# Dense projections as 512-column products with the tokens stationary

## The chip, the cores and the metric

The kernel runs on one core of a Trainium2 chip. The core has TensorE (PE, matrix products into PSUM banks), VectorE (DVE), ScalarE (ACT), GpSimd (POOL) and SyncE (SP, whose queue issues the transfers from memory). Each engine takes its own instructions in order, and semaphores hold an instruction until what it reads is there and what it overwrites has been read. The metric is the device time of one launch in microseconds.

## The reference

A block of a diffusion model over 256 latent tokens of width 1024, with 256 context tokens. What the change touches is the token mixer behind the input projection:

```python
z = h @ w_in            # 9 sections of 1024: q, i, f_fwd, f_bwd, og, u, v, gate_a, gate_b
# chunk_mlp: v normalised over its 1024 columns, mixed over 128 positions by w_s, times u
mu = jnp.mean(vf, axis=-1, keepdims=True)
vn = (vf - mu) * lax.rsqrt(var + EPS)
s = jnp.einsum('gtp,bnpgc->bntgc', w_s, vn) + b_s.T[:, :, None]
y_b = u * s
y_a = rms_norm(o, gnorm_g) * jax.nn.silu(og)      # o: two gated linear recurrences, 8 heads
merged = (jax.nn.sigmoid(gate_a) * (y_a @ w_branch_a)
          + jax.nn.sigmoid(gate_b) * (y_b @ w_branch_b))
x = x + g1 * (merged @ w_out)
# then: modulated norm, top 4 of 32 experts (clamped SwiGLU, 1024 wide), residual, norm
```

u and v pass through an exact GELU. The expert weights are 32 x 3 x 1024 x 1024 numbers of float32, and all of them are read.

## The kernel before

The work stands in five stages: start (modulation, first projections), attention in four pairs of heads with dense products in the gaps (heads 0 to 7), the middle (v, u, branch_b, gate and branch_a, w_out), the router, and 32 experts.

A dense product of float32 is made of three: `split` (L264) has ScalarE round a block to fp32r (`hi`, `ghi`) and DVE subtract it (`lo`, `glo`), and `dense` (L332) adds hi*hi, lo*hi and hi*lo. The class `Granule` (L311) is one weight block of 1024 x 256 in a 1 MB slot, and its `parts` splits four of its eight row tiles at a time, 128 x 1024 elements, into one of three buffers. With `natural` false the weights are stationary and the result is [channel, token]; with `natural` true the tokens are stationary, the weights stream past, and the result is [token, channel]. Either way one product here has 256 columns, except where latent and context tokens stream together (512). `two` (L349) makes a whole Granule's result in one PSUM bank (`acc`, two buffers). The other banks are `tp` (two buffers), `scores`, `o_ps`, `ua` and `ub` (one each).

v (L633) is natural; gate_b (L576, called `mb`), u (L649), branch_b (L669), gate (L662) and branch_a (L695) are [channel, token], so that the gated sum `m` can go as it is into w_out as its stationary operand; w_out (L703) is natural, and each quarter of its result goes into the residual `acc` and, turned, into the router. `mb` is the branch-b gate, made in the gaps of the last pair of heads, then multiplied by branch_b's product.

Weights are loaded by SP in program order into a rotation of slots: three of 1 MB (`ring`), and, from the third v block on (`LATER = 3`, L626), three of 2 MB (`ringb`). A load waits until the splits have read what was in its slot, and every load behind it waits with it. The first expert weights follow w_out in this queue (L69, L73). Later the experts have more slots.

What lies where on each engine is set by a scheduler from the program's dependences; the products of the attention and of the middle stage may pass each other on TensorE. `keep_busy` (L180) issues bf16 products of 512 columns that nobody reads.

Of the kernel before, what the change touches and what calls it, by code (L numbers as in the profile page):

```python
# [8 lines left out]
F32 = mybir.dt.float32  # L9
F32R = mybir.dt.float32r  # L10
BF = mybir.dt.bfloat16
I32 = mybir.dt.int32
AF = mybir.ActivationFunctionType
# [3 lines left out]
P = 128  # L17
D = 1024
# [13 lines left out]
def kernel(  # L32
# [295 lines left out]

    def win(sec, j, pieces=False):
        return Granule(w_in[0, :, sec * D + j * 256:sec * D + (j + 1) * 256], pieces)  # L330
# [236 lines left out]
    for j in range(5):  # L567
# [6 lines left out]
        else:  # L574
            mb = consts.tile([P, KT, T], F32, name="mb", tag="d1")
            steps = [lambda i=i: sc.activation(mb[:, 2 * i:2 * i + 2], two(win(8, i), hT[0], False), AF.Sigmoid)  # L576
                     for i in range(4)] + [lambda: None]
# [54 lines left out]
    for j in range(4):  # L632
        pp = two(win(6, j), hT[0], True)  # L633
        more_slots(j + 1)
        sc.activation(v[:, :, j * 256:(j + 1) * 256], pp, AF.Gelu)
# [26 lines left out]
    def gate(j):  # L662
        pp = two(win(7, j), hT[0], False)
        t = mid.tile([P, 2, T], F32, name="t2", bufs=2)
        sc.activation(t, pp, AF.Sigmoid)
        return t

    for j in range(4):
        pp = two(Granule(w_branch_b[0, :, j * 256:(j + 1) * 256]), (ybh, ybl), False)  # L669
        ve.tensor_mul(mb[:, 2 * j:2 * j + 2], mb[:, 2 * j:2 * j + 2], pp)  # L670
# [22 lines left out]
    for j in range(4):  # L693
        t = gate(j)
        pp = two(Granule(w_branch_a[0, :, j * 256:(j + 1) * 256]), (yhi, ylo), False)  # L695
        m = mid.tile([P, 2, T], F32, name="t3", bufs=2)
        ve.tensor_mul(m, pp, t)
        ve.tensor_add(m, m, mb[:, 2 * j:2 * j + 2])
        split(m, mhi[:, 2 * j:2 * j + 2], mlo[:, 2 * j:2 * j + 2])
# [3 lines left out]
    for j in range(4):  # L703
        s = slice(j * 256, (j + 1) * 256)
        g = Granule(w_out[0, :, s])
        t = mid.tile([P, 2, 256], F32, name="t3", bufs=2)
        if j < 3:
            pp = two(g, (mhi, mlo), True)
            ve.tensor_mul(t, pp, view(g1bc, j * 256, [[0, 2], [1, 256]]))
            ve.tensor_add(acc[:, :, s], acc[:, :, s], t)  # L710
        else:
            pps = [bank("acc") for _ in range(2)]
            dense(g, [(pps[tt][:, 0], tt, (mhi, mlo), True) for tt in range(2)], True)
            for tt in range(2):
# [375 lines left out]
```

## Time and profile before

| | us |
|---|---|
| median of three runs | 1432.9 (1430.99 to 1435.51) |
| profiled execution | 1439.14 |
| its span | 1437.4 |
| TensorE busy in the span | 1341.1 (93%) |
| DVE, ScalarE, POOL busy | 615.9, 306.2, 171.8 |

In the profile's rows times are microseconds from the start of the span. A row of a timeline has the start, the duration, the engine, the line, the operation, out<-in with the names of the tiles, and how often it stands in a row; in brackets the idle time before it and what ended it. Consecutive matmuls overlap, so their pace is read from starts, not from durations. For a product the operand that streams stands first behind the arrow and the stationary one second: `acc<-hh,ghi` has the weights stationary, `acc<-ghi,hh` the tokens.

### The profile page before, as it was taken

The numbers are of one execution on the slowest core, as the hardware profiler recorded it, in microseconds if no ns is written. First come the engines' busy times: TensorE is split into PE (matmuls) and PEld (weight loads), VectorE is DVE, ScalarE is ACT, GpSimd is POOL, SyncE is SP. The second block draws the span as 40 slices with busy tenths as digits, with TensorE's granted clock in tenths as the row PEclk, the third lists the DMA queues.
The fourth block names the chain that finished last, engine by engine and source line by source line (L and its number), as shares of the span: only waits on it lengthen the run. The fifth ranks groups of instructions, "written<-read, shape, count | busy, mean of one in ns | idle before, by whom it ended". The sixth has DMA issues, their size and how long they took to land. (4 is left out here: it accounts for less than half of the span.)

```text
span 1437.4 us, 18504 instructions
## 1 busy us (share of the span) xinstructions
PE 1341.1 (93%) x7806; PEld 727.7 (51%) x7806; DVE 615.9 (43%) x1100; ACT 306.2 (21%) x494; POOL 171.8 (12%) x147
## 2 busy tenths in 40 slices
PE   6988898989999999999999999989999899898986
PEld 3887787788999843333333332323323233232322
DVE  5597777768768522322322323213222232222214
ACT  3472545365444310000000000000000000010001
POOL 3045434240064000000000000000000000000001
PEclk8999999999999999999999999999999999999998
DMA  9645252534984899999999999999999999999994
GB/s 333 193 147 173 98 200 92 173 125 162 325 256 175 344 418 411 427 424 425 425 424 427 427 424 426 423 428 426 425 426 423 427 426 426 425 424 426 426 424 156
DMA packets 106882, 487.37 MB, mean 339 GB/s; under 512 B 6277, under 2 KB 64778, under 8 KB 77098
## 3 DMA queue, kind: packets, MB, share of 16 engines
q1 hardware_dynamic: 105946, 483.37, 83.9%
q0 software_dynamic: 848, 2.75, 0.6%
q8 instruction: 63, 1.03, 0.3%
q14 instruction: 25, 0.20, 0.0%
HBM read 485.06 MB, written 1.05 MB: 338 GB/s over the span
## 5 line engine op out<-in xcount | busy, mean ns | idle before, releaser
L827 PE MATMUL gate<-w,xT 128*64 128x512 f32 x1024 | 269.1, 604 | 13.4 <-DMA w<-in_w_dram 13.0
L827 PE MATMUL lin<-w,xT 128*64 128x512 f32 x1024 | 263.0, 592 | 0.0
L864 PE MATMUL py<-w,hT 128*64 128x512 f32 x992 | 227.2, 605 | 26.0 <-DMA w<-in_w_dram 25.9
L883 DVE SCALAR_TENSOR_TENSOR acc<-sc,wts,acc 128x512 f32<-128x512 f32 x122 | 86.0, 747 | 206.1 <-PE sc L880 206.1
L346 PE MATMUL acc<-hh,glo 128*128 128x256 f32 (+1 forms) x480 | 150.1, 314 | 7.3 <-DVE glo L266 7.3
L864 PEld LDWEIGHTS py<-w,hT 128*64 128x64 f32 x992 | 70.5, 139 | 162.5 <-issue 115.2
L266 DVE TENSOR_TENSOR glo<-w,ghi 128x1024 fp32r<-128x1024 f32 (+1 forms) x99 | 130.4, 1321 | 50.0 <-ACT ghi L265 49.7
L346 PE MATMUL acc<-hh,ghi 128*128 128x256 f32 (+1 forms) x480 | 151.6, 316 | 0.0
L346 PE MATMUL acc<-hl,ghi 128*128 128x256 f32 (+1 forms) x480 | 149.8, 312 | 0.0
L827 PEld LDWEIGHTS lin<-w,xT 128*64 128x64 f32 x1024 | 73.1, 137 | 146.6 <-issue 146.6
L827 PEld LDWEIGHTS gate<-w,xT 128*64 128x64 f32 x1024 | 62.6, 136 | 152.1 <-issue 103.5
L265 ACT ACTIVATE ghi<-w 128x1024 fp32r<-128x1024 f32 (+1 forms) x102 | 102.5, 1009 | 140.4 <-PE acc L346 109.0
L962 POOL DMA_DIRECT2D bc<-in_final_g_dram x1 | 0.6, 559 | 893.5 <-PE misc L809 893.5
L867 DVE TENSOR_TENSOR y<-py,g2h 128x512 f32<-128x512 f32 x31 | 21.4, 692 | 192.1 <-PE py L864 192.1
L346 PEld LDWEIGHTS acc<-hh,glo 128*128 128x128 f32 x480 | 95.1, 198 | 12.3 <-DVE glo L266 7.8
L346 PEld LDWEIGHTS acc<-hh,ghi 128*128 128x128 f32 x480 | 94.9, 198 | 4.5 <-issue 0.8
L346 PEld LDWEIGHTS acc<-hl,ghi 128*128 128x128 f32 x480 | 94.9, 198 | 4.2 <-issue 0.4
L802 ACT ACTIVATE xT<-misc,sh,a 128x128 f32<-128x128 f32 (+1 forms) x68 | 30.7, 452 | 276.7 <-DVE xT L804 276.7
L804 DVE TENSOR_SCALAR xT<-misc,a,sh 128x128 f32<-128x128 f32 (+1 forms) x68 | 27.3, 401 | 134.3 <-PE misc L798 123.7
L834 DVE TENSOR_SCALAR g<-gate 128x512 f32<-128x512 f32 x32 | 22.1, 692 | 138.2 <-PE gate L827 138.2
L835 ACT ACTIVATE s<-g 128x512 f32<-128x512 f32 x32 | 20.2, 630 | 282.7 <-DVE g L834 282.7
L798 PEld LDWEIGHTS misc<-p,acc 128*128 128x128 f32 x544 | 66.6, 196 | 26.6 <-issue 26.0
(323 smaller groups left out, 1696.4 us busy)
## 6 DMA issues: line engine op xcount, KB each, us to landing
w<-in_w_dram SPq DMA_DIRECT2D x148, 2048.0 KB, 29.5
w<-in_w_dram SPq DMA_DIRECT2D x88, 1024.0 KB, 31.5
w<-in_w_in_dram SPq DMA_DIRECT2D x33, 1024.0 KB, 5.1
w<-in_w_mod_dram SPq DMA_DIRECT2D x24, 1024.0 KB, 5.2
w<-in_w_branch_b_dram SPq DMA_DIRECT2D x4, 1024.0 KB
w<-in_w_branch_a_dram SPq DMA_DIRECT2D x4, 1024.0 KB, 11.8
w<-in_w_out_dram SPq DMA_DIRECT2D x4, 1024.0 KB, 10.3
w<-in_w_in_dram SPq DMA_DIRECT2D x12, 256.0 KB, 9.3
```

What stands on the lines that cost most here:

```text
L265: sc.activation(hi, src, AF.Copy)
L266: eng.tensor_sub(lo, src, hi)
L346: te.matmul(o, l, r, start=opens and kt == 0 and n == 0, stop=kt == KT - 1 and n == 2, skip_group_check=True)
L798: te.matmul(pg[:, k], view(x1, tt * D + kt // 2 * 256 + kt % 2, [[2, P]]), tok[:, tt], start=tt == 0, stop=tt == 1)
L802: sc.activation(xT[:, kt], pg[:, k], AF.Identity, bias=sh2[:, kt:kt + 1], scale=a2[:, kt:kt + 1])
L804: ve.tensor_scalar(xT[:, kt], pg[:, k], a2[:, kt:kt + 1], sh2[:, kt:kt + 1], op0=OP.mult, op1=OP.add)
L827: te.matmul(zz[n][h * C:(h + 1) * C], xT[:, kt], w[:, 0, n * D + h * 512:n * D + (h + 1) * 512], start=False, stop=kt == KT - 1, skip_grou ...
L834: ve.tensor_scalar(g, zz[0], 7.0, None, op0=OP.min)
L835: sc.activation(s, g, AF.Sigmoid, scale=1.702)
L864: te.matmul(py[h * C:(h + 1) * C], hT2[:, kt % 4, (kt // 4) * C:(kt // 4) * C + C], w[:, k, h * 512:(h + 1) * 512], start=False, stop=kt = ...
L867: ve.tensor_mul(y, py, g2h)
L883: ve.scalar_tensor_tensor(acc[:, tt, s], pcs[h], wcol[tt], old[:, tt, s], op0=OP.mult, op1=OP.add)
```

## The change

A new class `Wide` holds a weight block of 1024 x 512 as two halves of 512 rows, each in a 1 MB slot and each with its own load, and `wide` makes from it two results of [128 tokens, 512 channels] in two banks (`PAIRS`: the two `acc` buffers, or `scores` and `o_ps`), with the tokens stationary; two of the eight row tiles are split at a time, again 128 x 1024 elements. gate_b, v, branch_b, gate and branch_a, and the first half of w_out, go that way; `mb` becomes [token, channel]. The gated sum is made in `mb` and turned by sixteen TensorE transposes of 128 x 128 into the stationary operand of w_out. u and the last two quarters of w_out keep products of 256 columns. The gate's result now goes into a tile on `bsbc`'s place, and the 2 MB slots open after the second v block (`LATER = 2`).

```diff
--- before.py
+++ after.py
@@ -325,6 +325,32 @@
             lo = mid.tile([P, n, 256], F32R, name="glo", bufs=3)
             split(self.w[:, k0:k0 + n], hi, lo, eng)
             return hi, lo
+
+    class Wide:
+
+
+        def __init__(self, src):
+            self.w = []
+            for h in range(2):
+                self.w.append(wtile([P, 4, 512]))
+                nc.sync.dma_start(self.w[h], src[h * 512:(h + 1) * 512].rearrange("(k p) n -> p k n", p=P))
+
+        def parts(self, k0, n, eng=ve):
+            hi = mid.tile([P, n, 512], F32R, name="ghi", bufs=3)
+            lo = mid.tile([P, n, 512], F32R, name="glo", bufs=3)
+            split(self.w[k0 // 4][:, k0 % 4:k0 % 4 + n], hi, lo, eng)
+            return hi, lo
+
+    def wide(src, act, banks):
+
+        pps = [bank(n, (P, 512)) for n in banks]
+        dense(Wide(src), [(pps[tt], tt, act, True) for tt in range(2)], True, ((0, 2), (2, 2), (4, 2), (6, 2)))
+        return pps
+
+    def cols(j):
+        return slice(512 * j, 512 * j + 512)
+
+    PAIRS = ("acc", "acc"), ("scores", "o_ps")
 
     def win(sec, j, pieces=False):
         return Granule(w_in[0, :, sec * D + j * 256:sec * D + (j + 1) * 256], pieces)
@@ -572,9 +598,13 @@
             sg = [wk.tile([P, 2, 2 * T], F32, name=f"sg{h}", bufs=1) for h in range(2)]
             steps = pair_dense(j, iv, q, og, sg)
         else:
-            mb = consts.tile([P, KT, T], F32, name="mb", tag="d1")
-            steps = [lambda i=i: sc.activation(mb[:, 2 * i:2 * i + 2], two(win(8, i), hT[0], False), AF.Sigmoid)
-                     for i in range(4)] + [lambda: None]
+            mb = consts.tile([P, 2, D], F32, name="mb", tag="d1")
+
+            def gate_b(i):
+                pps = wide(w_in[0, :, 8 * D + 512 * i:8 * D + 512 * i + 512], hT[0], PAIRS[0])
+                for tt in range(2):
+                    sc.activation(mb[:, tt, cols(i)], pps[tt], AF.Sigmoid)
+            steps = [lambda: gate_b(0), lambda: None, lambda: gate_b(1), lambda: None, lambda: None]
         if prev:
             piv, pq, pog, psg = prev
             heads = []
@@ -629,10 +659,11 @@
     ve.scalar_tensor_tensor(a2, sc2, 1.0, n2col, op0=OP.add, op1=OP.mult)
 
     v = consts.tile([P, 2, D], F32, name="v", tag="big3")
-    for j in range(4):
-        pp = two(win(6, j), hT[0], True)
+    for j in range(2):
+        pps = wide(w_in[0, :, 6 * D + 512 * j:6 * D + 512 * j + 512], hT[0], PAIRS[j])
         more_slots(j + 1)
-        sc.activation(v[:, :, j * 256:(j + 1) * 256], pp, AF.Gelu)
+        for tt in range(2):
+            sc.activation(v[:, tt, cols(j)], pps[tt], AF.Gelu)
     st = late.tile([P, 2, 2, 6], F32, name="st")
     mv = late.tile([P, 2, 2], F32, name="mv")
     for tt in range(2):
@@ -659,15 +690,10 @@
         ve.tensor_mul(u, u, s.rearrange("p a b c -> p a (b c)"))
         split(u, ybh[:, 2 * j:2 * j + 2], ybl[:, 2 * j:2 * j + 2])
 
-    def gate(j):
-        pp = two(win(7, j), hT[0], False)
-        t = mid.tile([P, 2, T], F32, name="t2", bufs=2)
-        sc.activation(t, pp, AF.Sigmoid)
-        return t
-
-    for j in range(4):
-        pp = two(Granule(w_branch_b[0, :, j * 256:(j + 1) * 256]), (ybh, ybl), False)
-        ve.tensor_mul(mb[:, 2 * j:2 * j + 2], mb[:, 2 * j:2 * j + 2], pp)
+    for j in range(2):
+        pps = wide(w_branch_b[0, :, cols(j)], (ybh, ybl), PAIRS[j])
+        for tt in range(2):
+            ve.tensor_mul(mb[:, tt, cols(j)], mb[:, tt, cols(j)], pps[tt])
 
     b3 = consts.tile([96, 3, D], BF, name="b3", tag="attc")
     for k, src in ((0, b1[0, :, 0:D]), (1, b1[0, :, D:2 * D]), (2, b2[0])):
@@ -690,30 +716,35 @@
     gp.dma_start(acc, x[0].rearrange("(t p) d -> p t d", p=P))
 
     mhi, mlo = hT[1]
-    for j in range(4):
-        t = gate(j)
-        pp = two(Granule(w_branch_a[0, :, j * 256:(j + 1) * 256]), (yhi, ylo), False)
-        m = mid.tile([P, 2, T], F32, name="t3", bufs=2)
-        ve.tensor_mul(m, pp, t)
-        ve.tensor_add(m, m, mb[:, 2 * j:2 * j + 2])
-        split(m, mhi[:, 2 * j:2 * j + 2], mlo[:, 2 * j:2 * j + 2])
+    for j in range(2):
+        pps = wide(w_in[0, :, 7 * D + 512 * j:7 * D + 512 * j + 512], hT[0], PAIRS[0])
+        t = mid.tile([P, 2, 512], F32, name="ga", tag="bsbc")
+        for tt in range(2):
+            sc.activation(t[:, tt], pps[tt], AF.Sigmoid)
+        pps = wide(w_branch_a[0, :, cols(j)], (yhi, ylo), PAIRS[1])
+        for tt in range(2):
+            ve.tensor_mul(t[:, tt], t[:, tt], pps[tt])
+            ve.tensor_add(mb[:, tt, cols(j)], mb[:, tt, cols(j)], t[:, tt])
+        for i in range(2):
+            q = 2 * j + i
+            pt = bank("tp")
+            for k in range(2):
+                for tt in range(2):
+                    te.transpose(pt[:, k, tt * P:(tt + 1) * P], mb[:, tt, (2 * q + k) * P:(2 * q + k + 1) * P], ident)
+            split(pt, mhi[:, 2 * q:2 * q + 2], mlo[:, 2 * q:2 * q + 2])
 
     ss4 = late.tile([P, 2, 4], F32, name="ss4")
     pl = bank("ua", (P, 2, E))
-    for j in range(4):
+
+    def residual(s, pps):
+        for tt in range(2):
+            t = mid.tile([P, s.stop - s.start], F32, name="t3", bufs=2)
+            ve.tensor_mul(t, pps[tt], g1bc[:, s])
+            ve.tensor_add(acc[:, tt, s], acc[:, tt, s], t)
+
+    def routed(j):
+
         s = slice(j * 256, (j + 1) * 256)
-        g = Granule(w_out[0, :, s])
-        t = mid.tile([P, 2, 256], F32, name="t3", bufs=2)
-        if j < 3:
-            pp = two(g, (mhi, mlo), True)
-            ve.tensor_mul(t, pp, view(g1bc, j * 256, [[0, 2], [1, 256]]))
-            ve.tensor_add(acc[:, :, s], acc[:, :, s], t)
-        else:
-            pps = [bank("acc") for _ in range(2)]
-            dense(g, [(pps[tt][:, 0], tt, (mhi, mlo), True) for tt in range(2)], True)
-            for tt in range(2):
-                ve.tensor_mul(t[:, tt], pps[tt][:, 0], g1bc[:, s])
-                ve.tensor_add(acc[:, tt, s], acc[:, tt, s], t[:, tt])
         pt = bank("tp")
         for k in range(2):
             for tt in range(2):
@@ -735,6 +766,20 @@
             for tt in range(2):
                 te.matmul(pl[:, tt], h2[:, k, tt * P:(tt + 1) * P], wr_sb[:, kt], start=kt == 0 and tt == 0,
                           stop=kt == KT - 1, skip_group_check=True)
+
+    mix = (mhi, mlo)
+    residual(cols(0), wide(w_out[0, :, 0:512], mix, PAIRS[0]))
+    g2, g3 = (Granule(w_out[0, :, j * 256:(j + 1) * 256]) for j in (2, 3))
+    pp = bank("scores")
+    dense(g2, [(pp[:, tt], tt, mix, tt == 0) for tt in range(2)], True)
+    routed(0)
+    routed(1)
+    residual(slice(512, 768), [pp[:, tt] for tt in range(2)])
+    pps = [bank("acc") for _ in range(2)]
+    dense(g3, [(pps[tt][:, 0], tt, mix, True) for tt in range(2)], True)
+    routed(2)
+    residual(slice(768, 1024), [pps[tt][:, 0] for tt in range(2)])
+    routed(3)
 
     ss = sm2.tile([P, 2], F32, name="ss")
     ve.reduce_sum(ss, ss4, axis=mybir.AxisListType.X)
@@ -1058,7 +1103,7 @@
 WARM2 = (3, 12)
 RING_A = 3
 RING_B = 3
-LATER = 3
+LATER = 2
 RING_C = 2
 
 _INS = ['x', 'c', 'ctx', 'c_ctx', 'norm1_g', 'norm2_g', 'w_mod', 'b_mod', 'w_in', 'lb_fwd', 'lb_bwd', 'gnorm_g',
```

At the end of the attention, on TensorE: in the program before, head 7's last output products (`o_ps<-ks,lf`, L539, in the bank `o_ps`), then the dense products of v, and among them the transposes of the scaled output `on` (L556).

```order
L539 MATMUL o_ps<-ks,lf 64x128 x2
L535 MATMUL o_ps<-iv,attc 128x128 x2
L539 MATMUL o_ps<-ks,lf 64x128 x4
L346 MATMUL acc<-ghi,hh 128x256
...
L346 MATMUL acc<-ghi,hl 128x256
L556 MATMUL tp<-ident,on 128x128
L346 MATMUL acc<-glo,hh 128x256
L556 MATMUL tp<-ident,on 128x128
```

In the changed program the same place (L565 and L561 are the output products, L582 the transposes of `on`, L712 the router's base from `sh2`); v's second half writes `scores` and `o_ps`.

```order
L372 MATMUL scores<-ghi,hl 128x512
L372 MATMUL scores<-glo,hh 128x512
L712 MATMUL ub<-wr_sb,sh_71 128x32 x4
L565 MATMUL o_ps<-ks,lf 64x128 x2
L561 MATMUL o_ps<-iv,attc 128x128 x2
L565 MATMUL o_ps<-ks,lf 64x128 x4
L712 MATMUL ub<-wr_sb,sh_71 128x32 x4
L582 MATMUL tp<-ident,on 128x128 x2
L372 MATMUL o_ps<-ghi,hh 128x512
```

Before, 77 dense products stood between the last output and the first transpose of `on`; now only four small ones do, and 30 products of v, 24 of them into `o_ps`, stand behind the transposes.

In the u stage, on TensorE: before, the products of the position matrix with the normalised v (`o_ps<-wsT,v`, L655) come in groups of four behind 27 dense products each (the first group is cut by five dense ones).

```order
L655 MATMUL o_ps<-wsT,v 128x128 x3
L346 MATMUL acc<-hh,ghi 128x256
L346 MATMUL acc<-hl,ghi 128x256
...
L346 MATMUL acc<-hh,glo 128x256
L655 MATMUL o_ps<-wsT,v 128x128 x4
L346 MATMUL acc<-hh,ghi 128x256
```

In the changed program (L686 is that line now):

```order
L372 MATMUL acc<-hh,ghi 128x256
L686 MATMUL o_ps<-wsT,v 128x128
L372 MATMUL acc<-hl,ghi 128x256
L372 MATMUL acc<-hh,glo 128x256
...
L372 MATMUL acc<-hh,glo 128x256
L686 MATMUL o_ps<-wsT,v 128x128 x15
L372 MATMUL acc<-hh,ghi 128x256
```

All but the first of the sixteen now stand in a row behind u's first two blocks, in front of the 96 products of the third and the fourth block.

On POOL, in front of head 6's and head 7's small copies (L470, L471; L215, L216 and L221 multiply and add up a block of modulation weights, L452 and L479 are the heads' own): before

```order
L215 TENSOR_TENSOR w<-w,cs_163 128x2048
L452 TENSOR_SCALAR sg_2203<-sg_2203 128x2x256
L216 TENSOR_TENSOR w<-w 128x1024
L470 COPY w<-bl 128x8
L471 COPY w<-d_2862 128x8
L479 TENSOR_TENSOR cu<-cu,sg_2203 128x512
L221 TENSOR_TENSOR modrow<-w 128x512
```

and in the changed program

```order
L221 TENSOR_TENSOR modrow<-w 128x512
L478 TENSOR_SCALAR sg_2203<-sg_2203 128x2x256
L496 COPY w<-bl 128x8
L497 COPY w<-d_2862 128x8
L505 TENSOR_TENSOR cu<-cu,sg_2203 128x512
L215 TENSOR_TENSOR w<-w,cs_163 128x2048
L478 TENSOR_SCALAR sg_2204<-sg_2204 128x2x256
```

The block's multiply (L215) stood in front of head 6's work and now stands behind it, in front of head 7's. On SP, u's third block (L318) moved behind the fourth, the four halves of branch_b and one half of the gate.

## Rows read from the trace of the kernel before

**Rows 1.** The page: the span, and the busy share of the DMA engines (in tenths, 9 is 90% or more) and what they moved, in 40 equal slices of the span.

```profile
span 1437.4 us, 18504 instructions
...
DMA  9645252534984899999999999999999999999994
GB/s 333 193 147 173 98 200 92 173 125 162 325 256 175 344 418 411 427 424 425 425 424 427 427 424 426 423 428 426 425 426 423 427 426 426 425 424 426 426 424 156
```

**Rows 2.** Stretches of the span: its length, then busy time and instructions of TensorE, of its weight loads, DVE, ScalarE and POOL, the granted clock of TensorE, the DMA share and GB/s.

```profile
299.00:352.00 53.00, 48.97 (x440) 44.20 (x439) 41.52 (x72) 32.04 (x49) 20.46 (x17) 0.94 0.44 147
366.00:392.00 26.00, 26.00 (x224) 26.00 (x223) 20.35 (x35) 12.59 (x16) 0.00 (x0) 1.00 1.09 348
392.00:462.00 70.00, 69.07 (x595) 68.86 (x594) 52.94 (x41) 30.86 (x34) 39.82 (x28) 1.00 0.69 216
...
440.00:450.00 10.00, 9.07 (x77) 8.86 (x76) 10.00 (x5) 4.19 (x5) 8.93 (x5) 1.00 0.44 184
...
540.00:1437.00 897.00, 846.71 (x4001) 302.52 (x3997) 242.62 (x439) 69.06 (x133) 4.47 (x5) 0.99 0.98 414
```

**Rows 3.** Who waited for whom, TensorE's waits for expert weights: us in total, times, the longest.

```profile
PE py L864 <- DMA w<-in_w_dram: 25.9, 21, 3.0
...
PE gate L827 <- DMA w<-in_w_dram: 13.0, 22, 1.6
```

**Rows 4.** The timeline of SP's queue: three blocks of w_in, the first two expert loads, and four from 478.85 us.

```profile
361.13 2.24 SPq L318 DMA_DIRECT2D w<-in_w_in_dram  x3
...
438.11 13.65 SPq L69 DMA_DIRECT2D w<-in_w_dram  x2
...
478.85 2.05 SPq L73 DMA_DIRECT2D w<-in_w_dram  x4
```

**Rows 5.** The timeline of DVE at the end of w_out.

```profile
477.60 1.23 DVE L266 TENSOR_TENSOR glo<-w,ghi 128x1024 fp32r<-128x1024 f32 x1 [1.08 <-ACT ghi L265]
```

**Rows 6.** The timeline of TensorE: first and last of 21 dense products of 512 columns, of 74 of 256 columns, and of 24 of 256 columns, each without a gap.

```profile
206.96 0.39 PE L346 MATMUL acc<-hh,ghi 128*128 128x512 f32 x1
...
211.53 0.39 PE L346 MATMUL acc<-hh,glo 128*128 128x512 f32 x1
...
299.08 0.28 PE L346 MATMUL acc<-hh,ghi 128*128 128x256 f32 x1
...
307.36 0.28 PE L346 MATMUL acc<-hl,ghi 128*128 128x256 f32 x1
...
361.20 0.28 PE L346 MATMUL acc<-ghi,hh 128*128 128x256 f32 x1
...
363.91 0.28 PE L346 MATMUL acc<-glo,hh 128*128 128x256 f32 x1
```

**Rows 7.** The same view in the router: twelve bf16 products of 512 columns; one of them has a duration of 0.38 us.

```profile
490.75 2.75 PE L184 MATMUL ub<-onesb 128*128 128x512 bf16 x12
```

**Rows 8.** The same view in w_out: four transposes between dense products.

```profile
484.42 0.66 PE L720 MATMUL tp<-ident,acc 128*128 128x128 f32 x4
484.83 0.37 PE L346 MATMUL acc<-ghi,hl 128*128 128x256 f32 x1
485.04 0.28 PE L346 MATMUL acc<-glo,hh 128*128 128x256 f32 x1
```

**Rows 9.** The timelines of TensorE, DVE and POOL before head 6's scores: the pause, the first and the last of the four scans, and the multiply of modulation weights.

```profile
311.40 0.58 PE L346 MATMUL acc<-hh,glo 128*128 128x256 f32 x1 [3.77 <-DVE glo L266]
...
302.76 2.63 DVE L458 TENSOR_TENSOR_SCAN bl<-attc,lf 128x256 f32<-128x256 f32 x1 [1.39 <-ACT lf L450]
...
306.85 2.79 DVE L458 TENSOR_TENSOR_SCAN cu<-attc,lf 128x255 f32<-128x255 f32 x1
...
300.78 4.07 POOL L215 TENSOR_TENSOR w<-w,cs 128x2048 f32<-128x2048 f32 x1 [18.98 <-issue]
```

**Rows 10.** One stretch, behind that pause: length, TensorE's busy time and products, granted clock, DMA share, GB/s.

```profile
311.40:317.30 5.90, 5.89 (x27) 0.50 0.73 224
```

**Rows 11.** The timelines of ScalarE and DVE at the end of head 7: the square sums (L548) and v's first copy, the inverse root, a split among it, and the scaled output `on`.

```profile
351.09 0.28 ACT L548 ACTIVATE junk<-o_ps 128x128 f32<-128x128 f32 x1 [2.08 <-PE o_ps L539]
...
352.77 0.60 ACT L635 ACTIVATE v<-acc 128x512 f32<-128x512 f32 x1
353.27 0.27 ACT L548 ACTIVATE junk<-o_ps 128x128 f32<-128x128 f32 x1
...
353.66 0.17 DVE L103 TENSOR_SCALAR nv<-ss 128x2 f32<-128x2 f32 x1 [3.36 <-ACT junk L548]
...
354.62 1.23 DVE L266 TENSOR_TENSOR glo<-w,ghi 128x1024 fp32r<-128x1024 f32 x1
...
358.18 0.60 DVE L553 TENSOR_SCALAR on<-o_ps,rs 128x128 f32<-128x128 f32 x2
```

**Rows 12.** The timelines of TensorE and DVE in the u stage: a group of `wsT` products, and the add that frees its bank, the multiply and a split behind it.

```profile
383.31 1.05 PE L655 MATMUL o_ps<-wsT,v 128*128 128x128 f32 x8
...
380.32 0.69 DVE L658 TENSOR_TENSOR t<-o_ps,bsbc 128x512 f32<-128x512 f32 x1 [0.45 <-PE o_ps L655]
381.05 0.69 DVE L659 TENSOR_TENSOR t<-t,t 128x512 f32<-128x512 f32 x1
382.37 1.23 DVE L266 TENSOR_TENSOR glo<-w,ghi 128x1024 fp32r<-128x1024 f32 x1 [0.63 <-ACT ghi L265]
```

**Rows 13.** The page's list of transfers: w_in's blocks, how many, KB each, median us from issue to landing.

```profile
w<-in_w_in_dram SPq DMA_DIRECT2D x33, 1024.0 KB, 5.1
```

## The prediction

> **What bounds the kernel now.** I read the page's slices first [rows 1]. From the fifteenth slice on, the DMA line stands at 9 and the rate at 411 to 428 GB/s, to the end. The table of stretches [rows 2] shows what that means: from 540 to 1437 us TensorE is busy for 846.7 of 897 us, the DMA share is 0.98, and the two waits of TensorE that name an expert weight add up to 38.9 us [rows 3]. The experts run at the speed of the weight stream, and nothing in that part is edited.
>
> Then I asked when that stream becomes full. In SP's timeline [rows 4] two expert loads go out spread over 13.65 us from 438.11, as slots of the small rings come free; from 478.85 us four go out in 2.05 us. The last vector instruction before that is the split of the last w_out piece, 477.60 + 1.23 us [rows 5], which frees its slot. So what sets the end is the time at which the dense products of the middle stage give their slots back, and a microsecond there is a microsecond at the end.
>
> The middle stage is TensorE's: 26.0 of 26 us busy from 366 to 392 and 69.07 of 70 from 392 to 462, with one pause of 0.93 in the stretch 440 to 450. Only the stretch before it, 299 to 352, has idle time to give (48.97 of 53) [rows 2]. So the change is a sum over TensorE's time between 299 and 487 us: its instructions, their pace, and idle time that goes or comes.
>
> **The streams.** 1056 products of 256 columns become 528 of 512: all of gate_b, v, branch_b, gate and branch_a (192 each), and half of w_out's 192. Two paces of the narrow kind are in the trace: 74 rows from 299.08 to 307.36 us are 113.4 ns apart, 24 rows from 361.20 to 363.91 are 117.8 apart [rows 6]. I take the middle, 115.6, so 231.2 a pair. A 512-column product of the same split operands, with the weights stationary, takes 228.5 ns (21 rows from 206.96 to 211.53). So 528 x 2.7 = -1.4 us. The ends: 216 ns, the pace of twelve bf16 products of 512 columns ((2.75 - 0.38) / 11 [rows 7]), gives -8.0; twice the slower narrow pace, 235.6, gives +2.3. I choose 228.5, since it is the row with this kernel's operands.
>
> The Trainium skill (TensorE: Matmul & The Clock Gate, Back-to-back issue gap) gives an isolated warm product N/2.4 + 2.5 ns, so 215.8 at 512 columns. The bf16 rows agree; the rows at 228.5 do not. By that rule this term would be about -8, which is rival 4.
>
> **The transposes.** Four 128x128 transposes took from 484.42 to 484.83, and the product behind them then took 0.21 us to the next where 0.11 is usual [rows 8]: 0.51 us for four, 2.0 for the sixteen added. Ends: 1.8 (sixteen at 0.11) and 2.5 (a tenth more at each entry). TensorE being full there, they count: +2.0. Channel tiles 4 to 7 of the gated sum are turned last and wait for a multiply, an add, the transposes, a copy and a subtraction, with 24 narrow products of w_out (2.8 us) in between. I put 1.2 us of wait in place of today's 0.93: +0.3, between -0.9 and +2.
>
> **What goes: the stall before head 6.** TensorE stops for 3.77 us until 311.40 [rows 9]. The split it waits for stands on DVE behind the four scans of head 6, of which the first and the last took 2.63 and 2.79 us beside POOL's 4.07 us multiply of modulation weights. Then 27 products fill 5.9 us at a granted clock of 0.50 [rows 10], where 113 ns each would be 3.1: 2.8 more. In the changed order that multiply stands behind head 6's work on POOL, so I take all of it away: -6.6. If it stays, 0.
>
> **What comes: head 7's chain.** Now 77 products of v follow head 7's last output and hide its end [rows 11]: ScalarE's square sums at 351.09 and 353.27, with v's copy in between, small DVE operations from 353.66 with a 1.23 us split among them, the scaled output `on` from 358.18 (two of 0.60 together): 7.7 us from 351.09 to 358.78. After the change, v's second half writes the banks of the scores and of o_ps. The bank o_ps holds head 7's output, so 24 of v's last 30 products stand behind the transposes of `on`, and behind these on the same queue the whole u stage; the splits, and the slots that SP waits for, follow TensorE. The chain loses the split and gains a second copy of v (0.58) and 0.3 of statistics: about 7.4, of which 1.5 lie beside work still issued, and 0.3 go because the first half of `on` is enough. TensorE idles 5.6 us; between 1.5 (fill moved there by other waits) and 7.7. The one idle time of that size shown, the 3.77 us one, was followed by a granted clock of 0.50 [rows 10], so I add the same price, +2.8 (from 0). Together +8.4.
>
> **What comes: the u stage.** Now each group of `wsT` products stands behind 27 dense ones (the one at 383.31), so that the DVE add which frees the one o_ps bank (0.69) and the multiply and splits behind it are hidden [rows 12]. After the change fifteen of the sixteen products stand in a row. Each next group waits for an add, and DVE has between the adds a multiply of 0.69, then a subtraction and a multiply, then two splits of 1.23. The waits: 1.1 + 1.05 + 1.6 + 0.4 = 4.1 us, with the rest of u queued behind on TensorE. Ends: 1.4 (two adds' own time) and 7 (the splits wait in turn for ScalarE). +4.1.
>
> At nothing: ScalarE and DVE make as many splits of the same 128x1024 size, hidden as now; the loads bring the same bytes in rows of 2 KB in place of 1 KB; 528 weight loads fewer ran beside the products. The router tail after 487 us lies beside a stream that is full already. If that cover were gone, a late split would cost its own 1.23 us.
>
> **The sum.** -1.4 + 2.0 + 0.3 - 6.6 + 8.4 + 4.1 = +6.8 us on the profiled execution of 1439.14 us (span 1437.4): 1445.9. The median of the three timed runs, 1432.9, lies 6.2 below that execution, so 1439.7.
>
> **Rivals.**
> 1. The waits stay hidden (faster). If head 7's end and the u stage are covered, since products moved ahead let the heads run earlier, the sum is -1.4 + 2.0 + 0.3 - 6.6 = -5.7: 1427.2. For it: TensorE idles only 4.0 of 53 us there today [rows 2], so the attention is nearly filled and may end earlier. Against: the bank is a hard condition that slack does not soften.
> 2. Gains and waits cancel (no change): the clock holds and head 7 costs half, 6.8 - 2.8 - 2.8 = +1.2, 1434.1.
> 3. The load of u's third block comes late (slower still). In the changed order it stands on SP behind the fourth block, four halves of branch_b and one of the gate. Now it is one of three that go out from 361.13 us [rows 4], where the DMA moves 348 GB/s [rows 2], 3.0 us a megabyte; six more put it at about 380, and with the median 5.1 us to landing [rows 13] at 385, against a want at about 379. So +6: 1445.7. It decides from the point at which the queue, and not the slots, is late.
> 4. The streams run at 216 ns, -6.6 on the forecast: 1433.1.
>
> **Chances.** A measurement tells from no change what lies beyond 0.3%, 4.3 us. The forecast 0.40, rival 3 0.12, rival 1 0.24, rival 2 0.14, rival 4 0.10. Slower is the forecast and rival 3, 0.52; the same is rivals 2 and 4, 0.24; faster is rival 1, 0.24. The forecast's own range is 1436 to 1443. The whole range goes down to rival 1 and up to rival 3 with the 7 us end in the u stage (2.9 more), 1449.
>
> **What would show it.** 512-column products with tokens stationary 228 to 229 ns apart; no idle time of over 1 us before head 6's scores; an idle time of about 5.6 us before a transpose of `on`, and a granted clock of about 0.5 behind it; waits on an add before `wsT` products of 4 us in all; the last w_out split some 6.8 us later than 477.60, and the end as much later. The prediction is wrong if that split comes earlier than now, or if the end does not move with it.

## The result and the profile after

The changed kernel takes 1450.99 us, the median of four runs (1450.49 to 1451.81); the kernel before, run beside it, 1434.2 (1430.99 to 1437.52). The ratio is 1.0117, with a 95% interval of 1.0092 to 1.0143: slower, by 16.8 us. In a later comparison with 23 runs of the kernel before its median was 1435.5, which makes it 15.5. The forecast was slower by 6.8 us, so the direction was right and the size was less than half. The profiled execution of the changed kernel took 1451.48 us.

The page and the stretches come first, against [rows 1, 2] (in a stretch: its length; TensorE, weight loads, DVE, ScalarE and POOL busy; granted clock, DMA share, GB/s).

```profile
span 1449.7 us, 17478 instructions
...
DMA  9545253345865799999999999999999999999994
```

```profile
299.00:330.00 31.00, 27.06 (x155) 20.67 (x155) 28.46 (x35) 17.02 (x26) 20.19 (x13) 0.94 0.42 143
330.00:352.00 22.00, 19.64 (x138) 14.91 (x138) 15.07 (x33) 11.04 (x16) 1.00 (x2) 1.00 0.68 230
352.00:366.00 14.00, 8.54 (x56) 6.22 (x55) 6.93 (x25) 3.41 (x8) 1.32 (x3) 0.91 0.01 2
366.00:392.00 26.00, 23.75 (x152) 21.32 (x151) 16.08 (x32) 10.91 (x14) 0.00 (x0) 0.92 0.97 347
...
540.00:1437.00 897.00, 857.58 (x4074) 307.97 (x4070) 240.15 (x427) 68.15 (x128) 2.86 (x3) 1.00 1.00 419
```

The experts run as before, on a full DMA. What moved is the moment from which it is full. DVE's last split of w_out, and SP's queue beside it, answer to [rows 4, 5]:

```profile
490.88 1.22 DVE L266 TENSOR_TENSOR glo<-w,ghi 128x1024 fp32r<-128x1024 f32 x1
...
478.68 15.47 SPq L73 DMA_DIRECT2D w<-in_w_dram  x6
499.95 1.44 SPq L69 DMA_DIRECT2D w<-in_w_dram  x3
```

The split ends at 492.10 in place of 478.83, 13.3 us later, and the span is 12.3 longer. The stretch from 352 to 366 is the most striking: TensorE busy for 8.5 of 14 us, where in the kernel before it was busy throughout:

```profile
352.00:366.00 14.00, 14.00 (x124) 14.00 (x123) 10.28 (x23) 8.10 (x12) 0.00 (x0) 1.00 0.51 165
```

### The profile page after: what moved, and what is told of

Read it like the earlier page. It is cut to its first block, busy times and chain, and to the rows that moved or that the text cites. A ratio compares the mean times of both kernels' runs of the same rounds, so it can differ in the third digit from the quotient of the medians.

```text
span 1449.7 us, 17478 instructions
## 1 busy us (share of the span) xinstructions
PE 1347.7 (93%) x7294; PEld 706.7 (49%) x7294; DVE 617.4 (43%) x1102; ACT 304.4 (21%) x492; POOL 176.1 (12%) x147
## 3 DMA queue, kind: packets, MB, share of 16 engines
HBM read 485.06 MB, written 1.05 MB: 335 GB/s over the span
## 5 line engine op out<-in xcount | busy, mean ns | idle before, releaser
L909 PE MATMUL py<-w,hT 128*64 128x512 f32 x992 | 225.8, 602 | 25.7 <-DMA w<-in_w_dram 25.6
L372 PE MATMUL acc<-hh,glo 128*128 128x256 f32 (+1 forms) x288 | 94.4, 329 | 3.5 <-DVE glo L266 3.5
L372 PE MATMUL acc<-hh,ghi 128*128 128x256 f32 (+1 forms) x288 | 96.4, 335 | 0.0
L372 PE MATMUL acc<-ghi,hh 128*128 128x256 f32 (+1 forms) x256 | 87.2, 342 | 9.7 <-ACT hh L265 5.1
L372 PE MATMUL acc<-hl,ghi 128*128 128x256 f32 (+1 forms) x288 | 94.5, 328 | 0.0
L847 ACT ACTIVATE xT<-misc,sh,a 128x128 f32<-128x128 f32 (+1 forms) x68 | 30.7, 451 | 276.8 <-DVE xT L849 276.8
L372 PE MATMUL acc<-glo,hh 128*128 128x256 f32 (+1 forms) x256 | 83.7, 337 | 2.5 <-DVE glo L266 2.5
L372 PE MATMUL acc<-ghi,hl 128*128 128x256 f32 (+1 forms) x256 | 85.8, 335 | 0.0
## 6 DMA issues: line engine op xcount, KB each, us to landing
w<-in_w_dram SPq DMA_DIRECT2D x88, 1024.0 KB, 30.8
```

What stands on the lines that cost most here:

```text
L372: te.matmul(o, l, r, start=opens and kt == 0 and n == 0, stop=kt == KT - 1 and n == 2, skip_group_check=True)
L847: sc.activation(xT[:, kt], pg[:, k], AF.Identity, bias=sh2[:, kt:kt + 1], scale=a2[:, kt:kt + 1])
L909: te.matmul(py[h * C:(h + 1) * C], hT2[:, kt % 4, (kt // 4) * C:(kt // 4) * C + C], w[:, k, h * 512:(h + 1) * 512], start=False, stop=kt = ...
```

## Experiments

The first four versions change gate_b and v, in their form or in their banks. Each version has its own static order, so what an edit is worth includes what its order changed. In three comparisons, made at different times, the kernel before had medians of 1435.5 us (the first four versions), 1438.1 (the next four) and 1435.9 (the last four), so a difference of 2 or 3 us between versions of different comparisons tells nothing. Theory A was that the loss sits at the end of the attention, where gate_b and v are made; theory B that the wide form costs wherever it stands.

**v in the acc banks.** The changed kernel with

```diff
-        pps = wide(w_in[0, :, 6 * D + 512 * j:6 * D + 512 * j + 512], hT[0], PAIRS[j])
+        pps = wide(w_in[0, :, 6 * D + 512 * j:6 * D + 512 * j + 512], hT[0], PAIRS[0])
```

> The changed kernel, but v's second half goes into the two acc banks like its first, in place of the scores and o_ps banks. Theory A (the loss sits at the end of the attention: the o_ps bank makes v wait for head 7, and the u stage's small products bunch up behind it): the 5.5 us idle before the transposes of on and most of the half clock behind it go, and the three 0.78 us waits in the u stage: 7.4 + 2.3 less about 1 us that the acc banks' own copies cost, so 1442 us. Theory B (products of 512 columns with tokens stationary and the transposes cost wherever they stand): nothing goes, 1450 to 1451 us.

Measured: 1447.43 us (1445.55 to 1450.36). Between the two. The 5.46 us in front of `on` are gone and so are the u stage's three waits, but in their place TensorE waits for two others: in the timeline of this kernel,

```profile
352.66 1.94 PE L712 MATMUL ub<-wr_sb,sh 128*128 128x32 f32 x16 [2.60 <-issue]
...
359.74 0.79 PE L372 MATMUL acc<-ghi,hh 128*128 128x512 f32 x1 [2.44 <-ACT v L666]
```

In front of the second, v's second half waits until ScalarE has copied the first half out of the same two banks, behind a square sum and a table load. The profile names no releaser for the first; its products write the bank `ub`, and DVE's last operation that reads `ub` ends at 352.56.

**v narrow.** The changed kernel with the old loop over four 256-column blocks of v, and `LATER = 3`.

> The changed kernel with v as before: four blocks of 256 columns in the acc banks, and the 2 MB slots from the third block on. Theory A: as with v in the acc banks, or a little better, since one bank holds both token halves: 1441 us; the waits before head 7 (1.1 + 2.0 + 2.4 us and the half clock) stay. Theory B: v is 96 of the 528 wide products, so 96/528 of 16.8 us comes back: 1448 us.

Measured: 1443.3 us (1442.04 to 1444.74). 7.7 us come back: theory A's size less 2, and not B's 3. The waits before head 7 stayed, as expected of A. What A left out is a new wait for ScalarE's copy of v, at the end of head 7:

```profile
357.90 0.48 PE L372 MATMUL acc<-ghi,hh 128*128 128x256 f32 x1 [2.71 <-ACT v L665]
```

**gate_b narrow.**

```diff
+            steps = [lambda i=i: sc.activation(mb[:, :, i * 256:(i + 1) * 256], two(win(8, i), hT[0], True), AF.Sigmoid)
+                     for i in range(4)] + [lambda: None]
```

in place of the two wide steps; `mb` stays [token, channel].

> The changed kernel with the gate of branch b in four blocks of 256 columns, tokens stationary, in the acc banks; everything behind it stays wide. Theory A: the waits before head 7 (5.5 us idle and 1.4 us of half clock) go, but a stall before head 6's scores like that of the kernel before (3.8 us and 2.8 of half clock) may come back, and head 7's chain stays: 1444 to 1451 us, with an idle time of over 4 us before a transpose of on. Theory B: 96/528 of 16.8 us comes back: 1448 us.

Measured: 1445.36 us (1441.35 to 1447.01), in A's range. The stall before head 6 is back as it was in [rows 9], with 1.42 us more before head 6's scores, and those before head 7 are gone:

```profile
312.54 0.58 PE L372 MATMUL acc<-glo,hh 128*128 128x256 f32 x1 [3.74 <-DVE glo L266]
...
321.28 0.57 PE L522 MATMUL scores<-lf 128*32 128x64 f32 x32 [1.42 <-DVE lf L504]
```

But the idle time of over 4 us before a transpose of `on` that I expected at head 7's end did not come, though v's second half goes into the scores and o_ps banks here too. In this kernel's order 32 products of v (14 into acc, 18 into scores) stand between head 7's last output and the transposes of `on`, where the changed kernel has none. So the bank alone does not expose the chain; it is exposed where the order has used up v's first half and the scores half before.

**Both narrow.** Both edits together; branch_b, the gate, branch_a and half of w_out stay wide, with the transposes.

> The changed kernel with both the gate of branch b and v in blocks of 256 columns; branch_b, the gate, branch_a and half of w_out stay wide, and so do the sixteen transposes. Theory A: all of the loss but the transposes (2.0 us) and the pace (336 x 2 ns = 0.7 us) comes back: 1436 to 1438 us, with no idle time of over 1 us between head 7's last output and the end of w_out. Theory B: 336/528 of 16.8 us stays: 1445 us.

Measured: 1440.92 us (1437.53 to 1442.64), ratio 1.0030 (1.0014 to 1.0046). No idle time of over 1 us is left between head 7's last output and the end of w_out (the longest is 0.66), and ten of the 15 to 16 us come back: most of the loss is at the end of the attention, as A says. The rest, 4 to 5 us, is more than A's 0.7 + 2.0, so the time misses A's range, and the stall before head 6 stands there as in the kernel before (3.73 us).

**Turned, but narrow.** The kernel before, with both gates and both branch products as [token, channel] products of 256 columns (`two(..., True)`), and

```diff
+        pt = bank("tp")
+        for k in range(2):
+            for tt in range(2):
+                te.transpose(pt[:, k, tt * P:(tt + 1) * P], m[:, tt, k * P:(k + 1) * P], ident)
+        split(pt, mhi[:, 2 * j:2 * j + 2], mlo[:, 2 * j:2 * j + 2])
```

> The kernel before with both gates and both branch products in [token, channel] as products of 256 columns, and the gated sum turned by the same sixteen transposes; nothing is 512 columns wide. Theory (transposes 2.0 to 2.5 us, the rest of what the version with narrow gate_b and v kept is the wide products' pace and the loads in halves): 1437.5 to 1438. Rival (the layout alone makes the whole rest): as that version, 1440 to 1441.

Measured: 1438.41 us (1432.41 to 1439.58) beside 1438.11, ratio 1.0002 (0.9986 to 1.0019). Layout and transposes together cost about nothing that can be measured here (at most some 2.7 us): in this trace the last split ends at 479.8, 0.9 us later than before. Part of the transposes' cost is offset by the 0.93 us pause of the kernel before, which is not there. What both-narrow keeps above this version, 3.1 us at the last split (482.9), arises behind the u stage, whose last multiply starts at 395.08 here and at 395.06 there. Behind it both-narrow has the wide products, their loads in halves and another order of w_out's pieces. The pace explains about 1 us of the 3.1 (336 products, 233 ns in place of a pair's 230); the rest is not taken apart.

**Two banks for the u stage.** The changed kernel with

```diff
-        pss = bank("o_ps", (P, 2, 2, P))
+        pss = bank(("o_ps", "scores")[j % 2], (P, 2, 2, P))
```

> The changed kernel, with the wsT products of the u stage going into the o_ps and the scores bank in turn. Theory (one bank, freed by the add, makes each next group wait): the three idle times of 0.78 us shrink to under 0.1, -2.3 us, 1448.7. Rival (the groups wait for DVE's order, since the adds stand behind multiplies, subtractions and splits there): the same waits in front of later products, 1450.5 to 1451.

Measured: 1453.76 us (1452.37 to 1454.47), ratio 1.0105 to the kernel before where the changed kernel has 1.0117: no better. The rival holds: of the waits on the add one of 0.24 us is left, and the products behind the group wait instead, for a copy and for the split that stands on DVE behind the adds, 2.7 us in all where there were 2.3.

```profile
391.13 1.16 PE L686 MATMUL scores<-wsT,v 128*128 128x128 f32 x8 [0.24 <-DVE t L689]
393.94 0.38 PE L372 MATMUL acc<-hh,ghi 128*128 128x256 f32 x1 [1.65 <-ACT ghi L265]
395.26 0.39 PE L372 MATMUL acc<-hh,glo 128*128 128x256 f32 x1 [0.83 <-DVE glo L266]
```

**Modulation weights on DVE, in both kernels.** POOL multiplies and adds up half of each block of modulation weights in the attention's gaps. With

```diff
-MOD_POOL = (0,)
+MOD_POOL = ()
```

DVE does all of it. In the changed kernel:

> The changed kernel, with all modulation weights multiplied and added up on DVE and none on POOL. Theory (POOL's multiply stretches the scans of head 7 from 0.66 to about 3 us and so moves the old stall to a place before head 7): scans of 0.66 to 1.03, the waits of 1.1 and 2.0 us and the half clock behind them go, -4 to -5 us, 1446 to 1447. Rival (the waits come from the two acc banks and ScalarE's table loads, and DVE gets four more operations of 0.75 us for each of eight blocks): 1451 or slower.

Measured: 1420.89 us (1418.39 to 1422.29), ratio 0.9878 to the kernel before: 30 us less than the changed kernel, six times what I expected. The scans of heads 6 and 7 take 1.03 us at most, and the waits before head 7 are gone: from head 6's scores (0.49) to head 7's chain one idle time of 0.87 us is left. In the kernel before:

> The kernel before, with all modulation weights multiplied and added up on DVE and none on POOL. Theory: the scans of head 6 take 0.66 to 1.03 us, the 3.77 us stall and the half clock go, up to -6.6: 1429 to 1431. Rival: DVE, with 24 us more work in the attention, becomes what TensorE waits for there: 1435 or slower.

Measured: 1407.43 us (1406.45 to 1407.59), ratio 0.9787 (0.9768 to 0.9806): 30.7 us less than before. The expected 6 us were one head's stall; the gain builds up over the attention. The first scan of head 0 starts 0.5 us later than in the kernel before, that of head 2 9.5 earlier, of head 4 14.2, of head 6 25.7, and the last split ends 31.9 earlier. Between 60 and 350 us TensorE of the kernel before idles 29.5 us, 27.5 of them for DVE, 2.0 for ScalarE and none for POOL or a load. The two longest, which are gone with the modulation on DVE:

```profile
176.53 0.64 PE L496 MATMUL scores<-lf 128*32 128x64 f32 x10 [6.03 <-DVE lf L478]
244.69 0.85 PE L496 MATMUL scores<-lf 128*32 128x64 f32 x26 [6.97 <-DVE lf L478]
```

Of the 32.7 us by which the span is shorter, 22.4 are idle time of TensorE, and 10.3 are busy time of the same 7806 instructions, of which fewer run at half clock: between 60 and 350 us the granted clock is 0.99 in place of 0.94. Of DVE's scans (min/median/max in ns), first in the kernel before, then with the modulation on DVE:

```profile
L458 DVE TENSOR_TENSOR_SCAN bl<-attc,lf x16: 658/692/2893, 76.6 to 316.5; 128x256 f32<-128x256 f32 x16
```

```profile
L458 DVE TENSOR_TENSOR_SCAN bl<-attc,lf x16: 659/684/1717, 77.1 to 284.5; 128x256 f32<-128x256 f32 x16
```

The pair also tells what the change costs when both stalls before heads 6 and 7 are gone: 1420.89 less 1407.43 is 13.5 us. Of these, head 7's chain is there unchanged (in the changed kernel with the modulation on DVE):

```profile
334.39 0.66 PE L582 MATMUL tp<-ident,on 128*128 128x128 f32 x2 [5.34 <-DVE on L579]
```

**v narrow with the modulation on DVE.**

> The changed kernel with v in blocks of 256 columns and all modulation weights on DVE. Theory A (v in the o_ps bank costs the idle time at head 7's end, 5.3 us, 2 us of half clock behind it and the u stage's 2.3): against the changed kernel with the modulation on DVE, 1420.9 us, -9.6: 1411 to 1412. Theory B (the cost is spread over the wide products): -96/528 of 13.5, 1418.5.

Measured: 1409.5 us (1408.87 to 1410.59), 11.4 below the version with v wide. Theory A and not B. The two versions belong to different comparisons; each taken against the kernel before beside it, 9.1 us lie between them, so whether A's 9.6 was too low can't be told.

**Both narrow with the modulation on DVE.**

> The changed kernel with gate_b and v in blocks of 256 columns and all modulation weights on DVE; branch_b, the gate, branch_a and half of w_out stay wide. Theory A (behind the attention the wide form costs about 3 us: 336 products at 233.3 ns in place of pairs at 230.2, 1.0; transposes 1 to 2; the turned half's wait 0.7; and gate_b's wide form costs nothing but its pace once DVE and POOL don't collide): 1407.4 + 3 to 4 = 1410.5 to 1411.5, the same as with v alone narrow. Theory C (wide gate_b is what costs before head 7, by its two acc banks): over 4 us less than with v alone narrow.

Measured: 1411.86 us (1410.85 to 1414.2), near the expected range, and 2.4 above the version with only v narrow, so theory C falls: no cost of wide gate_b is left to see once the modulation is off POOL. Why it is a little better I did not settle; the version with it narrow has idle times of 1.98, 1.59 and 1.05 us that the other has not.

**All modulation on POOL.** The kernel before with `MOD_POOL = (0, 1)`.

> The kernel before with both halves of the modulation weights multiplied and added up on POOL. Theory (DVE and POOL stretch each other when both work, and the attention pays): taking POOL's half away gave -30 us, so a second half there gives +20 to +30: 1458 to 1468. Rival (what was gained came from POOL's late modulation sums holding SP's slots, not from DVE's stretched operations): scans and splits in the profile as long as before, and the time follows the slots, 1440 to 1450.

Measured: 1452.79 us (1451.09 to 1453.35), ratio 1.0108 (1.006 to 1.0156): +17, less than the expected 20 to 30, in the same direction, and above the rival's range. The operations are longer, against the rival: the longest scan of 256 columns goes from 2893 to 3803 ns. Held slots are in the traces too: SP's queue waits 47.8 us for POOL's sums in the kernel before and not at all with the modulation on DVE. But ScalarE, which rounds the blocks first, waits 7.1 us for blocks of w_in there and 6.3 with the modulation on DVE (60 to 360 us), so by these traces the slots explain little of the 30 us. Here it waits 16.5 us, and they can be part of the 17.

```profile
L458 DVE TENSOR_TENSOR_SCAN bl<-attc,lf x16: 656/692/3803, 77.1 to 326.8; 128x256 f32<-128x256 f32 x16
```

**Everything on DVE.** The kernel before with `MOD_POOL = ()`, and `gp` made `ve` in the four POOL operations of `decays`.

> The kernel before with all modulation weights, and the attention's four other POOL operations (the subtraction of one, two copies and the product with the decays), on DVE. Theory (any POOL operation beside DVE's stretches both): below 1407, by 3 to 8 us. Rival (DVE is now the fuller engine in the attention, and what is added on it, some 2 us a head, is waited for): 1407 to 1415.

Measured: 1405.07 us (1404.25 to 1405.93), ratio 0.978 (0.9734 to 0.9826), 2.4 below the version with only the modulation on DVE. But that belongs to another comparison: against the kernel before beside them the two gain 30.8 and 30.7 us, so the medians don't show what the four operations are worth. In the traces the last split ends 1.9 us earlier. It is the lowest median of all versions, 31 and 46 us below the two kernels. All scans now take the same time:

```profile
L458 DVE TENSOR_TENSOR_SCAN bl<-attc,lf x16: 664/682/695, 78.3 to 282.7; 128x256 f32<-128x256 f32 x16
```

## Why the prediction was right in direction and wrong in size

**The bound.** Right. In all fourteen profiles the time from the end of the last w_out split to the end of the span is the same, 956.5 to 958.6 us, while the split itself moves by 51 us:

| version | last split ends | span |
|---|---|---|
| before, all on DVE | 445.0 | 1402.5 |
| before, modulation on DVE | 446.9 | 1404.7 |
| changed, v narrow, modulation on DVE | 449.1 | 1407.5 |
| changed, both narrow, modulation on DVE | 452.3 | 1409.7 |
| changed, modulation on DVE | 461.4 | 1418.7 |
| before | 478.8 | 1437.4 |
| turned, narrow | 479.8 | 1437.4 |
| changed, both narrow | 482.9 | 1439.5 |
| changed, v narrow | 483.9 | 1441.2 |
| changed, gate_b narrow | 486.4 | 1443.7 |
| changed, v in the acc banks | 486.7 | 1445.0 |
| changed | 492.1 | 1449.7 |
| before, all modulation on POOL | 494.4 | 1450.9 |
| changed, two banks in the u stage | 495.8 | 1452.7 |

**The stall before head 6: the step that failed.** I wrote "In the changed order that multiply stands behind head 6's work on POOL, so I take all of it away: -6.6". It does stand behind head 6's, and the wait there is 0.77 us. But the multiply stands in front of head 7's scans, and there it does the same. The timelines of DVE, POOL, TensorE and ScalarE in the changed kernel:

```profile
300.48 0.68 DVE L484 TENSOR_TENSOR_SCAN bl<-attc,lf 128x256 f32<-128x256 f32 x1
...
312.50 3.02 DVE L484 TENSOR_TENSOR_SCAN bl<-attc,lf 128x256 f32<-128x256 f32 x1 [1.01 <-ACT lf L476]
...
316.97 2.79 DVE L484 TENSOR_TENSOR_SCAN cu<-attc,lf 128x255 f32<-128x255 f32 x1
...
310.28 4.69 POOL L215 TENSOR_TENSOR w<-w,cs 128x2048 f32<-128x2048 f32 x1 [2.97 <-DVE glo L266]
...
316.78 2.43 POOL L216 TENSOR_TENSOR w<-w 128x1024 f32<-128x1024 f32 x1
...
324.08 1.21 DVE L266 TENSOR_TENSOR glo<-w,ghi 128x1024 fp32r<-128x1024 f32 x1
...
325.32 9.86 SPq L336 DMA_DIRECT2D w<-in_w_in_dram  x4
...
308.64 0.57 PE L522 MATMUL scores<-lf 128*32 128x64 f32 x32 [0.77 <-DVE lf L504]
...
322.58 0.50 PE L372 MATMUL acc<-ghi,hh 128*128 128x512 f32 x1 [1.14 <-ACT ghi L265]
...
325.34 0.50 PE L372 MATMUL acc<-glo,hh 128*128 128x512 f32 x1 [2.03 <-DVE glo L266]
...
334.19 0.50 PE L372 MATMUL acc<-ghi,hh 128*128 128x512 f32 x1 [2.36 <-ACT mb L606]
...
330.22 2.01 ACT L265 ACTIVATE ghi<-w 128x1024 fp32r<-128x1024 f32 x2 [7.07 <-DMA w<-in_w_in_dram]
...
333.54 1.09 ACT L606 ACTIVATE mb<-acc 128x512 f32<-128x512 f32 x2
```

Head 6's first scan is at its 0.68, head 7's at 3.02 and its last at 2.79, the first beside POOL's multiply of modulation weights (L215) and the second beside the sum of the same block (L216). Head 7's exponentials on ScalarE are late, gate_b's last rounding and split behind them too (324.08), and TensorE waits 1.14 and 2.03 us; then, at a granted clock of 0.50, some eight products are 0.43 apart in place of 0.23 (1.6 us). The third wait, 2.36, goes back to the same split: when it ends, at 325.29, it frees the slot for v's first load (325.32), the load holds ScalarE until 330.22, and the copies of gate_b's results out of the two acc banks (333.54) stand behind it. That is 6.3 us idle and 1.6 of half clock where there were 3.8 and 2.8: +1.3 in place of -6.6, 7.9 us of the gap (0.8 of it the wait before head 6's scores, which is not the multiply's). My question stopped at the head from which the multiply was taken and did not follow it to where it went. So my sign, no idle time of over 1 us before head 6's scores, was met with 0.77 and told nothing. The version with the modulation on DVE bears the account out: head 7's scans take 1.03 us at most there, and the waits before head 7 are gone.

I had also misread [rows 9]: the multiply there ends at 304.85, so only head 6's first scan lies beside it. The last one, from 306.85, lies beside the sum:

```profile
306.66 2.43 POOL L216 TENSOR_TENSOR w<-w 128x1024 f32<-128x1024 f32 x1
```

**Head 7's chain.** The size was nearly right, 7.6 us in place of 8.4: 5.46 us of idle time against 5.6, and a granted clock of 0.66 over the next 6.5 us (2.1 us) against 2.8. The chain runs as worked out from [rows 11]: square sums before and after v's two copies, two statistics in front of the small operations.

```profile
359.32 0.28 ACT L574 ACTIVATE junk<-o_ps 128x128 f32<-128x128 f32 x1 [3.42 <-PE o_ps L565]
...
361.01 1.09 ACT L666 ACTIVATE v<-acc 128x512 f32<-128x512 f32 x2
361.98 0.28 ACT L574 ACTIVATE junk<-o_ps 128x128 f32<-128x128 f32 x1
...
361.64 1.29 DVE L671 BATCH_NORM_STATS2 st<-v 128x6 f32<-128x512 f32 x2 [1.18 <-ACT v L666]
362.84 0.15 DVE L103 TENSOR_SCALAR nv<-ss 128x2 f32<-128x2 f32 x1
...
365.19 0.61 DVE L579 TENSOR_SCALAR on<-o_ps,rs 128x128 f32<-128x128 f32 x2
...
365.69 0.66 PE L582 MATMUL tp<-ident,on 128*128 128x128 f32 x2 [5.46 <-DVE on L579]
```

But the reason that I gave, "the bank is a hard condition that slack does not soften", was too strong: with gate_b narrow the same banks stood behind the same chain, and 32 products hid it.

**The u stage.** The mechanism was right, the term too large: three waits of 0.78 us, 2.3 in all, against 4.1. I had let the third wait grow by the subtraction and the multiply, and added one for the splits; DVE reached each add as soon as the group was done, and the splits fell behind the last group.

```profile
388.22 1.16 PE L686 MATMUL o_ps<-wsT,v 128*128 128x128 f32 x8 [0.78 <-DVE t L689]
390.16 1.16 PE L686 MATMUL o_ps<-wsT,v 128*128 128x128 f32 x8 [0.78 <-DVE t L689]
...
389.41 0.69 DVE L689 TENSOR_TENSOR t<-o_ps,bsbc 128x512 f32<-128x512 f32 x1 [0.45 <-PE o_ps L686]
...
391.96 2.35 DVE L266 TENSOR_TENSOR glo<-w,ghi 128x1024 fp32r<-128x1024 f32 x2
```

**The streams.** Of the wrong sign: 48 products from 427.51 to 438.47 us are 233.2 ns apart, not 228.5, and in every profile here the wide products with the tokens stationary have that pace. Narrow ones in the same place of the turned-narrow version are 113 to 118 apart, 230 a pair. So 528 x 2 = +1.1 against -1.4, and 216 ns, rival 4, was never near. The rule of the Trainium skill that I weighed (TensorE: Matmul & The Clock Gate, Back-to-back issue gap; 215.8 ns is an estimate by its formula) is not borne out for these operands.

```profile
427.51 0.39 PE L372 MATMUL acc<-ghi,hh 128*128 128x512 f32 x1
...
438.47 0.39 PE L372 MATMUL acc<-glo,hh 128*128 128x512 f32 x1
```

**Transposes.** Right: the eight of the second half take from 478.78 to 479.86, the first eight 0.8 without the product between them, 1.9 in all against 2.0. No wait of over 0.5 us is left between the u stage and the end of w_out, where I had put 1.2 in place of 0.93. That pause I had put in the wrong place: it stood in front of a product of branch_a and had nothing to do with w_out's wait for the gated sum.

```profile
448.34 0.39 PE L346 MATMUL acc<-yhi,glo 128*128 128x256 f32 x1 [0.93 <-DVE glo L266]
```

In the changed kernel:

```profile
478.78 1.03 PE L733 MATMUL tp<-ident,mb 128*128 128x128 f32 x8
479.86 0.39 PE L372 MATMUL scores<-ghi,hh 128*128 128x256 f32 x1
```

**The sum.** As measured: +1.3, +7.6, +2.3, +1.1, +1.9 and -0.5 (the 0.93 pause, less one of 0.43), 13.7 us, against 13.3 at the last split. The spans differ by 12.3 us, so 3 to 4.5 us of the gap between the medians are not in these two traces: the profiled execution of the kernel before, 1439.14 us, was 3.7 above the median of 23 runs, and that of the changed kernel 0.5 above its own. I had carried the 6.2 us between the first profile and its median over to the changed kernel, where 0.5 are left. What makes the runs of the kernel before spread over 11 us and more, while those of the changed one and of the versions with the modulation on DVE stay within 1 to 4, stays open.

**The rivals.** Rival 3, the late load of u's third block, did not happen; the load that did come late was v's first, held by a slot (above). Rival 2 did not happen either: the clock fell, and head 7 cost nearly all that I had put. Rival 1 was wrong for the changed kernel, and right for the one with gate_b narrow, as far as head 7 goes.

## What to carry to other kernels

When an order moves an instruction away from a stall, look for what it stands beside next: the multiply that cost 6.6 us in front of head 6 cost some 7 in front of head 7, and the stall went for good only where the work left POOL. When a result that was spread over the gaps is made in fewer and larger pieces, count what is left to hide the long vector chain behind the last head, since the banks and the order decide that together. Where the bound is a stream behind a stage, one row, here the last split that frees a slot, tells what any edit in front of it is worth.

## What the runs showed of the hardware that I had not expected

Work on POOL beside DVE makes DVE late as well. Eight blocks' halves on POOL have their 62 us of operations there, and taking them off it, which adds 32 operations of 23 us together to DVE, made the whole kernel 30 us shorter; DVE's own busy time over the span went down, from 615.9 to 597.7 us. A scan of 256 columns of 0.66 us took up to 2.9 beside POOL's multiply or sum, 3.8 with twice the POOL work, and 0.70 at most with none of it beside the scans. The long scans have one thing in common: each of the six of over 2 us in the trace of either kernel ends 0.53 to 0.56 us after the end of a multiply or a sum on POOL that began before it. So the scan lasted as long as POOL's operation and then about its own time; why, no run here shows. And a product of 512 columns of these operands came every 233 ns with the tokens stationary and every 228 to 230 with the weights, wherever TensorE had its full clock and no gap, where two of 256 took 227 to 236: it gained next to nothing.
